# Last quarter of the second MLP product: weight-block sums formed by VectorE ahead of time and out of place, VectorE in program order from there on

## Chip, cores and metric

The kernel runs on one core of one Trainium2 chip. The metric is the device time of one execution in microseconds (us), as the median of the runs; lower is better.

## What is computed

One decoder layer on 512 tokens of width 1024, in fp32. After three token-mixer branches, the layer ends in an MLP with a squared ReLU, a residual sum and a last RMSNorm; only this end matters here:

```
hm = _rmsnorm(x, g_mlp)
x = x + jnp.square(jax.nn.relu(hm @ w_mlp_in)) @ w_mlp_out      # 1024 -> 4096 -> 1024
return _rmsnorm(x, g_final)
```

## The kernel before

**Precision.** Each fp32 matmul is done as three matmuls on parts: an operand is split into `hi` (ScalarE copies it, rounded, to a matmul format) and `lo` (VectorE subtracts: operand minus `hi`). `split_w` does this for weights (tiles `whi`, `wlo`, 128x1024 each, four buffers of each) and `stationary` for activations (`shi`, `slo`).

**The second MLP product** is cut into four quarters of the 4096 hidden channels (`prods[0]` to `prods[3]`). A quarter multiplies a 512x1024 activation block by a 1024x1024 weight block with seven block products in place of eight (`Product7`). The weight blocks are b11, b12, b21, b22 (`self.b[kh, nh]`, 128x4x512 each, tiles `wq`), loaded by DMA from SyncE's queue (SP). The seven products are issued in the order of `STEPS`: M1, M2, M5, M6, M7, M4, M3. M5 needs the weight sum t1 = b11+b12, M6 needs t2 = t1+b22, M7 needs t3 = b12+b22, M4 needs t4 = t2+b21; M1, M2, M3 take b11, b21, b22 as they are. M5, M6, M7 and M3 also need sums of activation blocks (tiles `u`, `sq`).

**PSUM banks.** Each product fills two banks (e = 0, 1). M1, M6, M7 and M4 pile up in the same pair "x", M2 has the pair "y", M5 and M3 the pair "z". After each product VectorE adds the bank into the residual `x2` (`add`; in the trace `x<-x,ps`). So the first matmul of M7 waits until VectorE has read what the bank held after M6, and the same holds for M4 after M7. M3, the last product, is computed in three pieces: bank e = 0, then the columns 0 to 255 and then 256 to 511 of bank e = 1, and each piece is added when it is done; the last piece waits for the add of the piece before it.

**Order of the work.** A product is two `parts` (kh = 0, 1: half of the weight block each). The list `parts` is worked through in order: the matmuls of part i are emitted, then the splits of part i+4. Between the products of quarters 0 to 2 stand parts of the first MLP product (`in_part`, 24 matmuls each), which need little of VectorE; in the last quarter there are none, and the 14 parts of `prods[3]` follow each other. A scheduler then decides where an engine's instruction stands in its order, unless it is pinned (`V.pin`, helper `_Engine`, line 95: every VectorE, ScalarE and GpSimd instruction has that line).

**Weight sums before.** In quarters 0 to 2 VectorE forms the sums in place in `prep`, one 128x2048 add each (`wq<-wq`). In the last quarter (`self.queue`) GpSimd's queue issues accumulating DMAs instead (`accumulate`, line 1010): they read a block from DRAM and add it to a block that lies in SBUF. One for t3 (on b12), two for t2, one for t1 (on b11, after M1's split), one for t4 (on t2, after M6's split).

**The end.** `final` (called by `add` for a quarter of the output at a time) squares the first half of a row on ScalarE with a sum (`jk`), folds it into `ss` on VectorE, and multiplies that half by the gain on GpSimd (`x<-x,gbf`). For the second half: ScalarE squares it (`hnx<-x`), VectorE completes `ss`, GpSimd takes the power -1/2 (`rsf`), ScalarE and VectorE scale the two halves, and SP stores them.

Of the kernel before, what the change touches and what calls it, by code (L numbers as in the profile page):

```python
# [11 lines left out]
F32 = mybir.dt.float32  # L12
F32R = mybir.dt.float32r
AF = mybir.ActivationFunctionType
ALU = mybir.AluOpType
AX = mybir.AxisListType

P = 128
# [121 lines left out]
def hybrid_block(ctx: ExitStack, tc: tile.TileContext, x, mem, g_mix, w_in, b_gate, conv_w, conv_b,  # L140
                 w_rg_a, b_rg_a, w_rg_x, b_rg_x, lru_lambda, w_lru_out, rel_bias, w_dil_out, g_mem,
                 w_mem_kv, w_mem_out, w_out, g_mlp, w_mlp_in, w_mlp_out, g_final, onehot, headsel, out):
    nc = tc.nc
# [403 lines left out]
    k0 = qk_proj(0, "k")  # L547
# [440 lines left out]
    class Product7:  # L988
# [3 lines left out]

        def __init__(self, w, k0, queue):
            self.queue = queue
            self.w, self.k0, self.b, self.ps, self.n = w, k0, {}, {}, 0

        def block(self, kh, nh):

            return cols(self.w, nh * 512, 512, self.k0 + kh * 4, 4)

        def load(self, kh, nh):
            b = self.b[kh, nh] = ml.tile([P, 4, 512], F32, name="wq", tag=f"wq{kh}{nh}")
            nc.sync.dma_start(b, self.block(kh, nh))
            if self.queue and (kh, nh) == (0, 1):
                self.accumulate(b, 1, 1)

        def accumulate(self, dst, kh, nh):
            nc.gpsimd.dma_start(out=dst, in_=self.block(kh, nh), accum_op=ALU.add)  # L1010

        def load_sum(self):

            self.t2 = raw_tile(4, 512)
            nc.sync.dma_start(self.t2, self.block(0, 0))
            self.accumulate(self.t2, 0, 1)
            self.accumulate(self.t2, 1, 1)

        def stationary(self, src):
            i, self.n = self.n, self.n + 1  # L1020
# [14 lines left out]
        def prep(self, p, sq):  # L1035

            b11 = self.b[0, 0]
            a11, a21 = (sq[0][:, :, h * 256:(h + 1) * 256] for h in range(2))
            if p == 1:
                self.stat = self.stationary(a11)  # L1040
                return b11
            b12, b21, b22 = (self.b.get(k) for k in ((0, 1), (1, 0), (1, 1)))
            a12, a22 = (sq[1][:, :, h * 256:(h + 1) * 256] for h in range(2))
            if p == 5:
                self.u = self.sums()
                V.tensor_sub(self.u, a21, a22)
                if not self.queue:
                    V.tensor_add(b11, b11, b12)
                act, w = self.u, b11
            elif p == 6:  # L1050
                u, self.u = self.u, self.sums()
                V.tensor_sub(self.u, u, a11)
                if self.queue:
                    b11 = self.t2
                else:
                    V.tensor_add(b11, b11, b22)
                act, w = self.u, b11
            elif p == 7:
                V.tensor_sub(a11, a11, a21)
                if not self.queue:  # L1060
                    V.tensor_add(b12, b12, b22)
                act, w = a11, b12
            elif p == 4:
                if self.queue:
                    b11 = self.t2
                else:
                    V.tensor_add(b11, b11, b21)
                act, w = a22, b11
            elif p == 3:
                V.tensor_add(self.u, self.u, a12)  # L1070
                act, w = self.u, b22
            else:
                act, w = a12, b21
            self.stat = self.stationary(act)
            return w
# [6 lines left out]
        def parts(self, n, sq, done, free):  # L1082


            p, bank, opens, (th, nh), sign = self.STEPS[n]
            last = n == 6 and done is not None
            now = {}

            def split(kh):
                if kh == 0:  # L1090
                    now["w"] = self.prep(p, sq)
                    now["a"] = self.stat
                now[kh] = split_w(now["w"][:, 2 * kh:2 * kh + 2, :], 2, 512)
                if kh == 1:
                    free(p)
                    if self.queue and p == 1:
                        self.accumulate(self.b[0, 0], 0, 1)
                    if self.queue and p == 6:
                        self.accumulate(self.t2, 1, 0)

            def mult(e, kh, c0, c1):
                (ah, al), (whi, wlo) = now["a"], now[kh]
                o = self.ps[bank, e][:, c0:c1]
                sl = slice(e * P, (e + 1) * P)
                for kk in range(2):
                    k = 2 * kh + kk
                    hi, lo = whi[:, kk, c0:c1], wlo[:, kk, c0:c1]
                    more = {"skip_group_check": not opens}
                    PE.matmul(o, ah[:, k, sl], hi, start=opens and k == 0, stop=False, **more)  # L1109
                    PE.matmul(o, ah[:, k, sl], lo, start=False, stop=False, **more)  # L1110
                    PE.matmul(o, al[:, k, sl], hi, start=False, stop=k == 3, **more)  # L1111

            def add(e, c0=0, c1=512):
                t = 2 * th + e
                v = x2[t][:, nh * 512 + c0:nh * 512 + c1]
                (V.tensor_add if sign > 0 else V.tensor_sub)(v, v, self.ps[bank, e][:, c0:c1])
                if done is not None and p in (2, 3, 7, 4):
                    done(t, nh, c0, c1)

            def multiply(kh):  # L1120
                if kh == 0 and opens:
                    for e in range(2):
                        self.ps[bank, e] = psum()
                if last:
                    if kh == 1:
                        for e, c0, c1 in ((0, 0, 512), (1, 0, 256), (1, 256, 512)):
                            mult(e, 0, c0, c1)
                            mult(e, 1, c0, c1)
                            add(e, c0, c1)
                    return  # L1130
                for e in range(2):
                    mult(e, kh, 0, 512)
                    if kh == 1:
                        add(e)

            return [(lambda kh=kh: split(kh), lambda kh=kh: multiply(kh)) for kh in range(2)]
# [49 lines left out]
    def in_part(q, n):  # L1186
        now = {}

        def split():
            m, e = q * 4 + n // 2, n % 2  # L1190
            now["w"] = split_w(raws[m][:, :, e * P:(e + 1) * P], KT, P)
            if e == 1:
                load_in(m + 2)
                if m == 14:
                    prods[3].load_sum()

        def multiply():
            ps = psum()
            mm3(ps, now["w"], hmmov, KT)
            hidden(q, n, ps)  # L1200
            if q == 0 and n in (2, 3, 4, 5):
                prods[0].load(*LOADS[n - 2])

        return now, split, multiply
# [5 lines left out]
    parts = [in_part(0, n)[1:] for n in range(2, 8)]  # L1210
    for q in range(4):
        def free(p, q=q):
            for b in FREE.get(p, ()) if q < 3 else ():
                prods[q + 1].load(*b)


        tiles = (2, 2, 1, 1, 1, 1, 0) if q == 2 else (1, 1, 1, 1, 1, 1, 2) if q < 2 else (0,) * 7
# [14 lines left out]
    for split, _ in parts[2:4]:  # L1232
        split()
    for i, (_, multiply) in enumerate(parts):
        multiply()
        if i + 4 < len(parts):
            parts[i + 4][0]()
# [27 lines left out]
```

## Time and profile before

| what | value |
|---|---|
| time of the runs | 875.82, 875.84, 877.86 us (median 875.84) |
| the profiled execution: its own time | 877.66 us |
| the profiled execution: its span | 875.8 us (1.86 us of its time lie outside) |
| TensorE busy | 855.3 us, 98% of the span |
| VectorE busy | 547.4 us, 63% |
| ScalarE busy | 387.8 us, 44% |
| mean granted TensorE clock | 0.991 |

TensorE (PE) is busy in nearly all of the span, so an engine that is idle elsewhere costs nothing there; what can still change is where TensorE waits, and how long the work after its last matmul takes. A row of a timeline gives the start, the duration, the engine and line, the operation with its tiles, and in brackets how long the engine was idle before and which instruction ended that. An instruction's duration reaches a little past the start of the next one on the same engine.

### The profile page before, as it was taken

How to read it: one execution, taken by the hardware profiler on the slowest of the kernel's cores; microseconds unless marked ns; L12 is line 12 of the kernel's file. 1: busy time of each engine (PE TensorE's matmuls, PEld its weight loads, DVE VectorE, ACT ScalarE, POOL GpSimd, SP SyncE). 2: the span in 40 equal slices, each digit the busy share in tenths (PEclk: the TensorE clock that was granted, in tenths of full speed). 3: DMA queues.
4: the chain of work that ended last, by engine and by line, in shares of the span. 5: the costliest groups of instructions: out<-in, count | busy, mean ns of one | idle time of the engine just before them, and what ended most of it. 6: DMA issues, size and time to landing. Idle time of an engine off the chain costs nothing.

```text
span 875.8 us, 10542 instructions
## 1 busy us (share of the span) xinstructions
PE 855.3 (98%) x4275; PEld 716.7 (82%) x4275; DVE 547.4 (63%) x700; ACT 387.8 (44%) x585; POOL 34.0 (4%) x39
## 2 busy tenths in 40 slices
PE   8899999999999999999999999999999999999986
PEld 7688888889888888888888889888888888888865
DVE  5769666764769642442523446488678856866785
ACT  5457566663654532242332225344425433444444
POOL 3110000000000000000000000000000000001022
PEclk9899999999999999999999999999999999999989
DMA  7583333215332232242325436512531442229522
GB/s 242 170 253 97 97 97 97 97 62 178 98 97 65 80 116 76 72 145 73 96 73 192 144 96 198 163 49 71 170 96 49 145 145 56 88 94 223 116 49 96
DMA packets 82332, 101.16 MB, mean 115 GB/s; under 512 B 3707, under 2 KB 64199, under 8 KB 82156
## 3 DMA queue, kind: packets, MB, share of 16 engines
q1 hardware_dynamic: 78444, 89.20, 32.3%
q0 software_dynamic: 3696, 10.77, 5.4%
q8 instruction: 33, 0.54, 0.3%
q10 hardware_dynamic: 144, 0.52, 0.2%
q14 instruction: 15, 0.12, 0.0%
HBM read 97.32 MB, written 5.52 MB: 117 GB/s over the span
## 4 chain that ended last, share of the span: by engine, by line
PE 85%; DVE 5%; DMA 4%; issue 2%; ACT 2%; POOL 0%; SPq 0%; POOLq 0%; ACTq 0%; DVEq 0%
PE ps L196 19%; PE ps L197 18%; PE ps L198 18%; PE ps L1109 4%; PE ps L1110 4%; PE ps L1111 4%; DMA wq<-in_w_mlp_out_dram 2%; DVE wlo L95 2%; PE ps L944 2%; PE ps L943 2%; PE ps L945 2%; PE ps L518 1%; PE ps L519 1%; PE ps L520 1%; DMA x<-in_x_dram 1%
## 5 line engine op out<-in xcount | busy, mean ns | idle before, releaser
L95 DVE TENSOR_TENSOR wlo<-raw,whi 128x1024 fp32r<-128x1024 f32 (+1 forms) x125 | 147.6, 1186 | 160.8 <-ACT whi L95 156.5
L95 ACT ACTIVATE whi<-raw 128x1024 fp32r<-128x1024 f32 (+1 forms) x126 | 129.4, 1030 | 230.9 <-PE ps L197 158.6
L196 PE MATMUL ps<-hT_hi,whi 128*128 128x512 f32 x400 | 156.6, 392 | 0.0
L197 PE MATMUL ps<-hT_lo,whi 128*128 128x512 f32 x400 | 155.8, 390 | 0.0
L198 PE MATMUL ps<-hT_hi,wlo 128*128 128x512 f32 x400 | 155.7, 389 | 0.0
L95 DVE TENSOR_TENSOR wlo<-wq,whi 128x1024 fp32r<-128x1024 f32 x52 | 65.3, 1257 | 59.5 <-ACT whi L95 59.5
L95 ACT ACTIVATE whi<-wq 128x1024 fp32r<-128x1024 f32 x52 | 54.9, 1058 | 102.4 <-PE ps L197 51.2
L1109 PE MATMUL ps<-whi,shi 128*128 128x512 f32 (+1 forms) x228 | 89.3, 392 | 5.6 <-DVE x L95 5.6
L197 PE MATMUL ps<-hmT_lo,whi 128*128 128x512 f32 x240 | 93.4, 389 | 0.0
L198 PE MATMUL ps<-hmT_hi,wlo 128*128 128x512 f32 x240 | 93.4, 389 | 0.0
L196 PE MATMUL ps<-hmT_hi,whi 128*128 128x512 f32 x240 | 93.2, 389 | 0.0
L1110 PE MATMUL ps<-wlo,shi 128*128 128x512 f32 (+1 forms) x228 | 88.8, 390 | 0.0
L1111 PE MATMUL ps<-whi,slo 128*128 128x512 f32 (+1 forms) x228 | 88.4, 388 | 0.0
L196 PEld LDWEIGHTS ps<-hT_hi,whi 128*128 128x128 f32 x400 | 75.1, 188 | 16.2 <-issue 0.6
L198 PEld LDWEIGHTS ps<-hT_hi,wlo 128*128 128x128 f32 x400 | 75.1, 188 | 15.7
L197 PEld LDWEIGHTS ps<-hT_lo,whi 128*128 128x128 f32 x400 | 75.1, 188 | 15.1
L1109 PEld LDWEIGHTS ps<-whi,shi 128*128 128x128 f32 x228 | 43.5, 191 | 15.5 <-issue 4.6
L198 PEld LDWEIGHTS ps<-hmT_hi,wlo 128*128 128x128 f32 x240 | 45.1, 188 | 9.4
L197 PEld LDWEIGHTS ps<-hmT_lo,whi 128*128 128x128 f32 x240 | 45.1, 188 | 9.3
L196 PEld LDWEIGHTS ps<-hmT_hi,whi 128*128 128x128 f32 x240 | 45.0, 188 | 9.2
L1110 PEld LDWEIGHTS ps<-wlo,shi 128*128 128x128 f32 x228 | 43.5, 191 | 8.7
L1111 PEld LDWEIGHTS ps<-whi,slo 128*128 128x128 f32 x228 | 43.3, 190 | 8.8
(254 smaller groups left out, 1353.2 us busy)
## 6 DMA issues: line engine op xcount, KB each, us to landing
raw<-in_w_in_dram SPq DMA_DIRECT2D x23, 1024.0 KB
raw<-in_w_mlp_in_dram SPq DMA_DIRECT2D x16, 1024.0 KB
wq<-in_w_mlp_out_dram SPq DMA_DIRECT2D x16, 1024.0 KB
raw<-in_w_in_dram SPq DMA_DIRECT2D x12, 512.0 KB
raw<-in_w_mem_kv_dram SPq DMA_DIRECT2D x4, 1024.0 KB
raw<-in_w_out_dram SPq DMA_DIRECT2D x4, 1024.0 KB
x<-in_x_dram SPq DMA_DIRECT2D x7, 512.0 KB
raw<-in_w_lru_out_dram SPq DMA_DIRECT2D x4, 768.0 KB
```

The lines of the kernel that those rows point to most:

```text
L95: r = fn(*a, **k)
L196: PE.matmul(ps, whi[:, k0 + k, :], ah, start=k == 0, stop=False)
L197: PE.matmul(ps, whi[:, k0 + k, :], al, start=False, stop=False)
L198: PE.matmul(ps, wlo[:, k0 + k, :], ah, start=False, stop=k == nk - 1)
L518: PE.matmul(ps[:, 0:256], ah, hi[:, k % 4, :], start=k == 0, stop=False)
L519: PE.matmul(ps[:, 0:256], ah, lo[:, k % 4, :], start=False, stop=False)
L943: PE.matmul(ps, ah[:, sl], hi[:, k % 2, :], start=k == 0, stop=False)
L944: PE.matmul(ps, ah[:, sl], lo[:, k % 2, :], start=False, stop=False)
L945: PE.matmul(ps, al[:, sl], hi[:, k % 2, :], start=False, stop=k == KT - 1)
L1109: PE.matmul(o, ah[:, k, sl], hi, start=opens and k == 0, stop=False, **more)
L1110: PE.matmul(o, ah[:, k, sl], lo, start=False, stop=False, **more)
L1111: PE.matmul(o, al[:, k, sl], hi, start=False, stop=k == 3, **more)
```

## The change

In the last quarter the five accumulating DMAs and the second load of b11 are gone. VectorE forms the four sums instead, each into a tile of its own or into b12, and all of them while the third quarter's last products run: `block_sums(0)` (t1, t3) when M4 of the third quarter has been split, `block_sums(1)` (t2) when the last part of the first MLP product has been split, `block_sums(2)` (t4) when M3 of the third quarter has been split. b22 is loaded earlier, into a spare activation buffer (`wx`). Besides, VectorE's instructions are pinned in program order over the last 14 parts; inside `final` they are not.

```diff
-        def load(self, kh, nh):
-            b = self.b[kh, nh] = ml.tile([P, 4, 512], F32, name="wq", tag=f"wq{kh}{nh}")
+        def load(self, kh, nh, dst=None):
+            b = self.b[kh, nh] = dst or ml.tile([P, 4, 512], F32, name="wq", tag=f"wq{kh}{nh}")
             nc.sync.dma_start(b, self.block(kh, nh))
-            if self.queue and (kh, nh) == (0, 1):
-                self.accumulate(b, 1, 1)
-
-        def accumulate(self, dst, kh, nh):
-            nc.gpsimd.dma_start(out=dst, in_=self.block(kh, nh), accum_op=ALU.add)
-
-        def load_sum(self):
-
-            self.t2 = raw_tile(4, 512)
-            nc.sync.dma_start(self.t2, self.block(0, 0))
-            self.accumulate(self.t2, 0, 1)
-            self.accumulate(self.t2, 1, 1)
+
+        def block_sums(self, step, dst):
+            b11, b12, b21, b22 = (self.b[k] for k in ((0, 0), (0, 1), (1, 0), (1, 1)))
+            if step == 0:
+                self.t1, self.t3 = dst, b12
+                V.tensor_add(dst, b11, b12)
+                V.tensor_add(b12, b12, b22)
+            elif step == 1:
+                self.t2 = dst
+                V.tensor_add(dst, self.t1, b22)
+            else:
+                self.t4 = dst
+                V.tensor_add(dst, self.t2, b21)
...
                 if kh == 1:
                     free(p)
-                    if self.queue and p == 1:
-                        self.accumulate(self.b[0, 0], 0, 1)
-                    if self.queue and p == 6:
-                        self.accumulate(self.t2, 1, 0)
...
                 if done is not None and p in (2, 3, 7, 4):
+                    pin, V.pin = V.pin, False
                     done(t, nh, c0, c1)
+                    V.pin = pin
...
                 load_in(m + 2)
-                if m == 14:
-                    prods[3].load_sum()
+                if m == 15:
+                    prods[3].block_sums(1, raw_tile(4, 512))
...
         def free(p, q=q):
-            for b in FREE.get(p, ()) if q < 3 else ():
+            if q == 2 and p == 7:
+
+                prods[3].load(1, 1, ml.tile([P, 4, 512], F32, name="wx", tag="sq", bufs=4))
+            for b in FREE.get(p, ()) if q + (p == 3) < 3 else ():
                 prods[q + 1].load(*b)
+            if q == 2 and p == 4:
+                prods[3].block_sums(0, raw_tile(4, 512))
+            if q == 2 and p == 3:
+                prods[3].block_sums(2, ml.tile([P, 4, 512], F32, name="wx", tag="sq", bufs=4))
...
     for i, (_, multiply) in enumerate(parts):
+        V.pin = i >= len(parts) - 14
         multiply()
```

What this does to VectorE's order is seen at three places. In the rows, `x2_4030`, `x2_4032`, `x2_4034`, `x2_4036` are the four 128-token blocks of the residual, and the numbers tell tiles apart.

First, VectorE before, from the last split of a first-MLP weight (`wlo_6223`) on, while the third quarter ends:

```order
L95 TENSOR_TENSOR wlo_6223<-raw_5922,whi_6221 128x1024
L95 TENSOR_TENSOR wlo_6259<-wq_5664,whi_6257 128x1024
L95 TENSOR_TENSOR sq_6101<-sq_6101 128x512
L95 TENSOR_TENSOR wlo_6275<-wq_5664,whi_6273 128x1024
L95 TENSOR_TENSOR x2_4034<-x2_4034,ps_5819 128x512
```

The same place in the changed kernel (`wq_6200` is b11, `wq_6128` b12, `wx_6126` b22, `wq_6202` b21):

```order
L95 TENSOR_TENSOR wlo_6223<-raw_5922,whi_6221 128x1024
L95 TENSOR_TENSOR raw_6204<-wq_6200,wq_6128 128x2048
L95 TENSOR_TENSOR wlo_6261<-wq_5664,whi_6259 128x1024
L95 TENSOR_TENSOR wq_6128<-wq_6128,wx_6126 128x2048
L95 TENSOR_TENSOR raw_6225<-raw_6204,wx_6126 128x2048
L95 TENSOR_TENSOR sq_6097<-sq_6097 128x512
L95 TENSOR_TENSOR wlo_6277<-wq_5664,whi_6275 128x1024
L95 TENSOR_TENSOR wx_6279<-raw_6225,wq_6202 128x2048
L95 TENSOR_TENSOR x2_4034<-x2_4034,ps_5819 128x512
```

Four 128x2048 sums have come in between the same splits and adds.

Second, VectorE before, between the splits of M6 and the first add of M6 (`x2_4030<-x2_4030,ps_6371`, which M7's first matmul waits for); `slo_6482` and `wlo_6487`, `wlo_6505` belong to M7, `slo_6520` and `wlo_6525` to M4:

```order
L95 TENSOR_TENSOR wlo_6463<-raw_6072,whi_6461 128x1024
L95 TENSOR_SCALAR ss0_0_6444<-ss0_0_6444 128x1
L95 TENSOR_TENSOR slo_6482<-sq_5884,shi_6481 128x1024
L95 TENSOR_SCALAR ss0_1_6456<-ss0_1_6456 128x1
L95 TENSOR_TENSOR wlo_6487<-wq_6130,whi_6485 128x1024
L95 TENSOR_TENSOR x2_4034<-x2_4034,ps_6466 128x512
L95 TENSOR_TENSOR x2_4036<-x2_4036,ps_6467 128x512
L95 TENSOR_TENSOR wlo_6505<-wq_6130,whi_6503 128x1024
L95 TENSOR_TENSOR slo_6520<-sq_6101,shi_6519 128x1024
L95 TENSOR_TENSOR x2_4030<-x2_4030,ps_6371 128x512
```

In the changed kernel M6's splits end with `wlo_6464`, and M6's first add is `x2_4030<-x2_4030,ps_6372`:

```order
L95 TENSOR_SCALAR ss0_0_6445<-ss0_0_6445 128x1
L95 TENSOR_TENSOR x2_4032<-x2_4032,ps_6415 128x512
L95 TENSOR_SCALAR ss0_1_6457<-ss0_1_6457 128x1
L95 TENSOR_TENSOR wlo_6464<-raw_6225,whi_6462 128x1024
L95 TENSOR_TENSOR sq_5884<-sq_5884 128x4x256
L95 TENSOR_TENSOR slo_6482<-sq_5884,shi_6481 128x1024
L95 TENSOR_TENSOR wlo_6487<-wq_6128,whi_6485 128x1024
...
L95 TENSOR_TENSOR wlo_6505<-wq_6128,whi_6503 128x1024
L95 TENSOR_TENSOR slo_6520<-sq_6097,shi_6519 128x1024
L95 TENSOR_TENSOR wlo_6525<-wx_6279,whi_6523 128x1024
L95 TENSOR_TENSOR x2_4030<-x2_4030,ps_6372 128x512
```

The two `ss0` steps now stand between and behind the adds of M2, the activation sum `sq_5884` stands right ahead of the `slo_6482` that is made from it, and M4's first weight split `wlo_6525` stands ahead of M6's first add; left out are the two adds of M5.

Third, VectorE before in M3, from the last scaling of block 3 on (`x2_4030<-x2_4030,ps_6466` adds the piece e = 0, the 128x256 adds the two pieces of e = 1):

```order
L95 SCALAR_TENSOR_TENSOR hnx_6630<-x2_4036,rsf_6634,gbf_4367 128x512
L95 TENSOR_TENSOR x2_4030<-x2_4030,ps_6466 128x512
L95 TENSOR_TENSOR x2_4032<-x2_4032,ps_6467 128x256
L95 SCALAR_TENSOR_TENSOR ss0_0_6444<-s1_6654,ss0_0_6444 128x1
L95 SCALAR_TENSOR_TENSOR hnx_6653<-x2_4030,rsf_6657,gbf_4367 128x512
L95 TENSOR_TENSOR x2_4032<-x2_4032,ps_6467 128x256
```

The same place in the changed kernel:

```order
L95 SCALAR_TENSOR_TENSOR hnx_6630<-x2_4036,rsf_6634,gbf_4367 128x512
L95 TENSOR_TENSOR x2_4030<-x2_4030,ps_6466 128x512
L95 SCALAR_TENSOR_TENSOR ss0_0_6445<-s1_6654,ss0_0_6445 128x1
L95 SCALAR_TENSOR_TENSOR hnx_6653<-x2_4030,rsf_6657,gbf_4367 128x512
L95 TENSOR_TENSOR x2_4032<-x2_4032,ps_6467 128x256
L95 SCALAR_TENSOR_TENSOR ss0_1_6457<-s1_6677,ss0_1_6457 128x1
L95 TENSOR_TENSOR x2_4032<-x2_4032,ps_6467 128x256
```

The first 128x256 add now stands behind the finishing of block 0 (`ss0_0`, `hnx_6653`).

## Rows read from the trace of the kernel before

**Rows 1.** The page: busy time of TensorE, share of the span, instructions.
```profile
PE 855.3 (98%) x4275; PEld 716.7 (82%) x4275; DVE 547.4 (63%) x700; ACT 387.8 (44%) x585; POOL 34.0 (4%) x39
```

**Rows 2.** TensorE's waits from 560 us on: us in total, times, longest.
```profile
PE ps L1109 <- DVE x L95: 5.6, 2, 4.3
```

**Rows 3.** Timeline of TensorE, last quarter.
```profile
842.97 0.39 PE L1111 MATMUL ps<-whi,slo 128*128 128x512 f32 x1
847.61 0.77 PE L1109 MATMUL ps<-whi,shi 128*128 128x512 f32 x1 [4.25 <-DVE x L95]
...
853.04 0.39 PE L1110 MATMUL ps<-wlo,shi 128*128 128x512 f32 x1
...
866.92 0.39 PE L1109 MATMUL ps<-whi,shi 128*128 128x256 f32 x1 [1.33 <-DVE x L95]
```

**Rows 4.** Windows: length, busy time (instructions) of each engine, clock, DMA share, GB/s.
```profile
804.80:829.20 24.40, 24.40 (x110) 20.20 (x109) 15.40 (x17) 11.37 (x12) 1.27 (x1) 1.00 0.71 162
829.20:847.60 18.40, 14.16 (x63) 11.42 (x62) 18.23 (x20) 8.32 (x11) 4.60 (x3) 0.96 0.33 58
845.00:850.00 5.00, 2.39 (x6) 1.93 (x7) 3.02 (x4) 1.64 (x2) 0.00 (x0) 0.60 0.55 100
```

**Rows 5.** SP's timeline: loads of b12 and of b11.
```profile
788.63 0.37 SPq L1005 DMA_DIRECT2D wq<-in_w_mlp_out_dram  x1
...
799.51 0.37 SPq L1005 DMA_DIRECT2D wq<-in_w_mlp_out_dram  x1
```

**Rows 6.** GpSimd's timeline: an accumulating DMA, a multiplication of `final`.
```profile
794.07 1.30 POOL L1010 DMA_DIRECT2D wq<-in_w_mlp_out_dram  x1 [1.58 <-DMA wq<-in_w_mlp_out_dram]
...
837.72 2.05 POOL L95 TENSOR_TENSOR x<-x,gbf 128x512 f32<-128x512 f32 x1 [17.85 <-ACT jk L95]
```

**Rows 7.** VectorE's timeline: a weight sum; the end of the third quarter; first add of M1.
```profile
778.89 2.28 DVE L95 TENSOR_TENSOR wq<-wq 128x2048 f32<-128x2048 f32 x1
...
818.93 1.22 DVE L95 TENSOR_TENSOR u<-sq 128x1024 f32<-128x1024 f32 x1
...
829.20 1.28 DVE L95 TENSOR_TENSOR x<-x,ps 128x512 f32<-128x512 f32 x2
```

**Rows 8.** ScalarE's timeline: M1's first split behind b11's load; a split behind an activation sum.
```profile
811.93 1.06 ACT L95 ACTIVATE whi<-wq 128x1024 fp32r<-128x1024 f32 x1 [2.82 <-DMA wq<-in_w_mlp_out_dram]
...
820.19 1.06 ACT L95 ACTIVATE shi<-u 128x1024 fp32r<-128x1024 f32 x1 [0.20 <-DVE u L95]
```

**Rows 9.** VectorE's timeline: up to M6's first add, and the split after it.
```profile
838.59 2.26 DVE L95 TENSOR_TENSOR slo<-sq,shi 128x1024 fp32r<-128x1024 f32 x1
...
840.84 2.57 DVE L95 TENSOR_TENSOR wlo<-wq,whi 128x1024 fp32r<-128x1024 f32 x1
843.33 1.27 DVE L95 TENSOR_TENSOR x<-x,ps 128x512 f32<-128x512 f32 x2
844.53 1.21 DVE L95 TENSOR_TENSOR wlo<-wq,whi 128x1024 fp32r<-128x1024 f32 x1
845.66 1.21 DVE L95 TENSOR_TENSOR slo<-sq,shi 128x1024 fp32r<-128x1024 f32 x1
846.80 0.67 DVE L95 TENSOR_TENSOR x<-x,ps 128x512 f32<-128x512 f32 x1
849.45 1.23 DVE L95 TENSOR_TENSOR wlo<-raw,whi 128x1024 fp32r<-128x1024 f32 x1 [1.98 <-ACT whi L95]
```

**Rows 10.** VectorE's timeline: the end.
```profile
859.82 0.67 DVE L95 TENSOR_TENSOR x<-x,ps 128x512 f32<-128x512 f32 x1
861.34 0.16 DVE L95 SCALAR_TENSOR_TENSOR ss<-s,ss 128x1 f32<-128x1 f32 x1 [0.85 <-ACT hnx L95]
862.16 0.75 DVE L95 SCALAR_TENSOR_TENSOR hnx<-x,rsf,gbf 128x512 f32<-128x512 f32 x1 [0.67 <-POOL rsf L95]
...
865.86 1.01 DVE L95 TENSOR_TENSOR x<-x,ps 128x512 f32<-128x512 f32 x2
...
870.68 0.75 DVE L95 SCALAR_TENSOR_TENSOR hnx<-x,rsf,gbf 128x512 f32<-128x512 f32 x1 [0.66 <-POOL rsf L95]
```

More of the change, by code (lines that the diff above doesn't have):

```diff
@@ L988, in hybrid_block, with __init__ @@
     class Product7:
-        def __init__(self, w, k0, queue):
-            self.queue = queue
+        def __init__(self, w, k0, last):
+            self.last = last
             self.w, self.k0, self.b, self.ps, self.n = w, k0, {}, {}, 0
@@ L1046, in prep @@
                 V.tensor_sub(self.u, a21, a22)
-                if not self.queue:
+                if not self.last:
                     V.tensor_add(b11, b11, b12)
-                act, w = self.u, b11
+                act, w = self.u, self.t1 if self.last else b11
             elif p == 6:
@@ L1052, in prep @@
                 V.tensor_sub(self.u, u, a11)
-                if self.queue:
-                    b11 = self.t2
-                else:
+                if not self.last:
                     V.tensor_add(b11, b11, b22)
-                act, w = self.u, b11
+                act, w = self.u, self.t2 if self.last else b11
             elif p == 7:
                 V.tensor_sub(a11, a11, a21)
-                if not self.queue:
+                if not self.last:
                     V.tensor_add(b12, b12, b22)
@@ L1063, in prep @@
             elif p == 4:
-                if self.queue:
-                    b11 = self.t2
-                else:
+                if not self.last:
                     V.tensor_add(b11, b11, b21)
-                act, w = a22, b11
+                act, w = a22, self.t4 if self.last else b11
             elif p == 3:
```

## The prediction, as it was put on record

> **What bounds the kernel now.** First the page: TensorE is busy in 98% of the span [rows 1], so work on another engine counts only where TensorE waits for it, or behind the last matmul. Then TensorE's waits in the last 316 us: two, 5.6 us together, both for a VectorE add [rows 2]. The timeline shows where: 4.25 us before M7's first matmul and 1.33 us before the last piece of M3 [rows 3]. Behind the first one the granted clock is 0.60 in the window from 845 to 850 us, which mixes the half level (1.2 GHz) with the full one, and the pace is back only by 853.04 [rows 3, 4]. Last, VectorE itself: from 829.20 to 847.60 it is busy for 18.23 of 18.40 us [rows 4]. So the tail is VectorE's chain of instructions, worked through in order, and I price the change by walking that chain before and after. The marks are the starts of four adds: M1's first (829.20), M6's first (846.80), M3's first (865.86) and the last scaling (870.68) [rows 7, 9, 10]; 5.1 us of span follow the last mark in both kernels.
>
> **Unit prices.** What counts in a chain is the distance to the next start: 1.14 us for a 128x1024 operation (845.66 to 846.80), 0.60 for a 128x512 add (two from 843.33 to 844.53) [rows 9], 2.20 for a 128x2048 sum, its 2.28 less the same overlap of 0.08 [rows 7]. Three round trips matter when nothing stands between their ends in VectorE's order. Activation sum, ScalarE's split, VectorE's `slo`: the sum starts at 818.93, the split ends at 821.25, VectorE itself would be free 1.14 after its start, so it idles 1.2 us [rows 7, 8]. Add, ScalarE's square, `ss`: 0.85 us of idling. `ss`, GpSimd's power, VectorE's scaling: 0.67 [rows 10].
>
> **The change, part by part.**
>
> *The loads.* b11 is still requested when M4 of the third quarter has been split, at 799.51 [rows 5]. Before, ScalarE got it at 811.93, 12.4 us later, with accumulating DMAs under way [rows 8]. b12's load had the DMA engines nearly to itself: requested at 788.63, the accumulate that waits for it starts at 794.07, at most 5.4 us later [rows 5, 6]. Those are the bounds. Without the accumulates nothing else is queued at 800 us, so I take 5.3 us: b11 is there at 804.8. b12, b21 and b22 are requested before it.
>
> *The sums.* The first sum needs b11, and VectorE works in order, so its chain starts at 804.8. Up to M1's first add it holds four sums (8.8 us), ten 128x1024 splits and sums (11.4) and six 128x512 operations (3.6): 23.8 us, plus one activation round trip of 1.2 (`u_6386` is followed directly by its `slo_6389`). M1's first add starts at 829.8, 0.6 us later than before. What hides the 8.8 us is idle time of VectorE: it worked for only 15.40 of the 24.40 us in this stretch [rows 4]. That cover is nearly used up, and each further microsecond would count in full. **+0.6**
>
> *The order up to M6's first add.* Before, this takes 17.6 us: ten 128x1024 operations, six adds, two `ss` steps are 15.1, and the other 2.5 are two operations stretched from 1.22 to 2.26 and 2.57 [rows 9], beside GpSimd's multiplications of `final` [rows 6]. After, it holds eleven 128x1024 operations, because M4's split `wlo_6525` now stands ahead of the add: 16.3. To that come waits that the pinned order makes. `u_6428` is followed directly by `slo_6431`: 1.2. Each `ss0` now stands right behind the add whose square it needs: twice 0.85. `sq_5884` stands directly ahead of `slo_6482`; before, six instructions lay between: 1.2. Of GpSimd's two multiplications the first now falls on VectorE's wait for the second square, the other stretches `wlo_6464` by about 1.2. Together 21.6 us, so M6's first add starts at 851.4 instead of 846.80 and M7's first matmul, 0.81 behind it as before, at 852.2 instead of 847.61. TensorE reaches that point as early as before or a little later (M6's second half waits about 1.5 us for the stretched `wlo_6464`), so its idle time before M7 is some 7 us, not 4.25. **+4.0**
>
> On that stretch the Trainium skill has a rule (SBUF — State Buffer, § SBUF: two separate sides): a VectorE operation with two SBUF inputs and a GpSimd operation that reads SBUF exclude each other for a whole instruction. By it a GpSimd multiplication of 2.05 us could hold VectorE for all of that; the first stretched row lost 1.04. With 2.05 at each of the two places where I charge 1.2, the sum would be 1.7 us higher; I go by the rows.
>
> *M6's first add to M3's first add.* Before 19.1 us. After: five 128x1024 operations, six adds, four `ss` steps and two scalings are 10.9. Waits: one activation round trip (1.2); `wlo_6564`, whose `whi` needs the buffer that M7's first half gives back (M7 starts at half rate, 0.43 us a matmul, so about 1.4); `ss0_2`, whose square stands on ScalarE behind a split that waits for M7's second half (about 1.6); `ss0_3` (0.85); one GpSimd multiplication (1.2); twice square and power for blocks 2 and 3 (3.1). Together 20.3. The 1.98 us that VectorE lost before to the last accumulate [rows 9] are gone, but these waits stand in their place. **+1.2**
>
> *The last piece of M3.* Before, the 128x256 add that frees the bank follows M3's first add by 0.60 [rows 10]. After, `ss0_0` and `hnx_6653` stand between, with both their round trips: 0.60 + 0.85 + 0.08 + 0.67 + 0.67 = 2.9. **+2.3**. Before that piece TensorE then idles about 5.5 us, longer than the 4.25 that were followed by half rate, so I charge its twelve 128x256 matmuls half rate, 0.22 for 0.12 us, 1.2 in all, less 0.2 for an add that no longer stands behind a scaling. **+1.0**
>
> *At no cost:* GpSimd's five DMA issues and the second read of b11 off SP's queue; nobody waited for either on this chain except as named.
>
> Sum: 0.6 + 4.0 + 1.2 + 2.3 + 1.0 = 9.1 us. The profiled execution took 877.66 (span 875.8), so a like one would take 886.8; it is one of the slower of the executions shown. On the median of 875.84 the sum gives **885.0 us**.
>
> **Rivals.**
>
> *The waits shrink, the kernel gets faster.* The mechanism is VectorE's order itself: if ScalarE and GpSimd answer while VectorE still has other work, only the instruction times are left. M6's first add would start at 828.6 + 16.3 = 844.9, 1.9 us earlier than before; TensorE's idle time of 2.3 us might then leave the clock at full, and M7, M4 and M3 would run at TensorE's pace (48 and 18 matmul times of 0.227 us from 845.7 to 860.7), the last scaling near 865.3: 870.5 us. It decides at the pairs: of some 17 us of waits that I count from 829.8 on, about 9 would have to vanish before the change breaks even. For it speaks that before, idle VectorE time is short there. Against it, the order puts sum and `slo`, add and `ss` next to each other, and a ScalarE split alone takes 1.06 [rows 8]. Chance 0.07; near no change, with half of the waits gone, 0.04.
>
> *b11 arrives as late as before.* Then the chain starts at 811.9 and not at 804.8, and as it has no slack left all 7.1 us count: 892.1. For it: that is the only load of b11 that the trace shows. Against it: what filled the DMA engines then (share 0.71 over that stretch [rows 4]) is what the change removes. Chance 0.08.
>
> *The dearer estimates fail.* GpSimd's multiplications fall on gaps (2.4 us less) and TensorE is not slowed at half rate behind its stalls (1.2 for the last piece, about 2 for M7): 885.0 - 5.6 = 879.4. For it: two of four multiplications are already charged nothing; the 1.33 us wait was not followed by half rate [rows 3]. Against it: the stalls grow past the one that was. Chance 0.15.
>
> **How the numbers follow.** My forecast (883 to 888 us) has 0.66, the three others 0.11, 0.08 and 0.15. The range leaves out the first rival and most of the second, 0.19 together: 879.4 to 890.0. A measurement of this kernel tells a change from none at about 0.3%, 2.6 us. Slower by more: 0.66 + 0.08 + 0.15 = 0.89; same 0.04; faster 0.07.
>
> **What would show it.** In the changed kernel's trace: the first 128x2048 sum starts near 804.8, directly behind its DMA; M1's first add near 829.8; TensorE's wait before M7 near 7 us, ended by `x<-x,ps`, and M7 starting near 852; short VectorE waits for ScalarE behind `u`, `sq` and the adds; a wait before the last piece of 5 us or more. I am wrong if M7 starts before 848, if the sums run past 820, or if the 128x256 add does not wait for GpSimd's power.

## The result, and the profile after

The changed kernel takes 885.72 us in the median of four runs (885.20 to 886.22), the kernel before 876.75 in the four that ran beside it: ratio 1.0106, 95% interval 1.0090 to 1.0121, so 9 us slower. The forecast was 885.0, in a range from 879.4 to 890.0. The profiled execution took 885.2 us, with a span of 883.2.

The page of the changed kernel: busy time of the engines, against [rows 1].

```profile
PE 854.6 (97%) x4275; PEld 716.5 (81%) x4275; DVE 556.0 (63%) x704; ACT 388.0 (44%) x585; POOL 24.1 (3%) x34
```

VectorE has 8.6 us more work, which is about the four sums (2.28 us each), and TensorE's work is the same within 0.7 us. TensorE's waits from 560 us on, against [rows 2]:

```profile
PE ps L1102 <- DVE x L95: 12.8, 2, 7.4
PE ps L1103 <- DVE wlo L95: 1.3, 1, 1.3
```

Still two waits for an add of VectorE, but 12.8 us instead of 5.6; the third is for a weight split. TensorE's timeline shows the places, which answer to [rows 3]:

```profile
840.98 0.50 PE L1103 MATMUL ps<-wlo,shi 128*128 128x512 f32 x1 [1.31 <-DVE wlo L95]
850.90 0.76 PE L1102 MATMUL ps<-whi,shi 128*128 128x512 f32 x1 [7.36 <-DVE x L95]
...
873.68 0.58 PE L1102 MATMUL ps<-whi,shi 128*128 128x256 f32 x1 [5.43 <-DVE x L95]
```

The second half of M6 waits for the stretched `wlo`, M7 waits 7.36 us in place of 4.25, the last piece of M3 5.43 in place of 1.33. Two windows that answer to [rows 4], the second from M1's first add to M6's first add of this kernel:

```profile
804.80:829.20 24.40, 24.40 (x109) 20.19 (x108) 23.27 (x22) 11.08 (x12) 0.00 (x0) 1.00 0.00 1
828.05:850.07 22.02, 14.19 (x62) 11.09 (x60) 17.69 (x20) 10.43 (x13) 2.59 (x2) 0.95 0.00 1
```

Around M1's first add VectorE went from 15.40 to 23.27 us of 24.40: the sums filled its idle time. (The first window has the times of [rows 4], while M1's first add is at 828.05 here; the 24.40 us that end there have the same 23.27.) In the second window VectorE is busy for 17.69 of 22.02 us, where before it was busy for nearly all of that stretch, 18.23 of 18.40: now it waits. The DMA share is 0.00 where it was 0.71 and 0.33.

VectorE's timeline of the changed kernel, the rows that answer to [rows 7, 9, 10]:

```profile
800.47 1.22 DVE L95 TENSOR_TENSOR wlo<-raw,whi 128x1024 fp32r<-128x1024 f32 x1
803.07 2.29 DVE L95 TENSOR_TENSOR raw<-wq 128x2048 f32<-128x2048 f32 x1 [1.38 <-DMA wq<-in_w_mlp_out_dram]
...
825.77 1.23 DVE L95 TENSOR_TENSOR slo<-u,shi 128x1024 fp32r<-128x1024 f32 x1 [1.13 <-ACT shi L95]
...
828.05 1.28 DVE L95 TENSOR_TENSOR x<-x,ps 128x512 f32<-128x512 f32 x2
...
833.20 1.23 DVE L95 TENSOR_TENSOR slo<-u,shi 128x1024 fp32r<-128x1024 f32 x1 [1.60 <-ACT shi L95]
...
836.95 0.15 DVE L95 TENSOR_SCALAR ss<-ss 128x1 f32<-128x1 f32 x1 [0.79 <-ACT jk L95]
837.02 0.68 DVE L95 TENSOR_TENSOR x<-x,ps 128x512 f32<-128x512 f32 x1
838.51 0.15 DVE L95 TENSOR_SCALAR ss<-ss 128x1 f32<-128x1 f32 x1 [0.81 <-ACT jk L95]
838.58 2.35 DVE L95 TENSOR_TENSOR wlo<-raw,whi 128x1024 fp32r<-128x1024 f32 x1
840.85 1.21 DVE L95 TENSOR_TENSOR sq<-sq 128x1024 f32<-128x1024 f32 x1
843.19 1.23 DVE L95 TENSOR_TENSOR slo<-sq,shi 128x1024 fp32r<-128x1024 f32 x1 [1.13 <-ACT shi L95]
...
850.07 1.28 DVE L95 TENSOR_TENSOR x<-x,ps 128x512 f32<-128x512 f32 x2
...
870.20 0.68 DVE L95 TENSOR_TENSOR x<-x,ps 128x512 f32<-128x512 f32 x1
871.72 0.16 DVE L95 SCALAR_TENSOR_TENSOR ss<-s,ss 128x1 f32<-128x1 f32 x1 [0.84 <-ACT hnx L95]
872.54 0.75 DVE L95 SCALAR_TENSOR_TENSOR hnx<-x,rsf,gbf 128x512 f32<-128x512 f32 x1 [0.66 <-POOL rsf L95]
873.21 0.42 DVE L95 TENSOR_TENSOR x<-x,ps 128x256 f32<-128x256 f32 x1
...
878.47 0.75 DVE L95 SCALAR_TENSOR_TENSOR hnx<-x,rsf,gbf 128x512 f32<-128x512 f32 x1 [0.66 <-POOL rsf L95]
```

Start times of two traces can't be compared directly: how much time lies ahead of the changed part varies from trace to trace by up to 2.8 us. So each mark is counted from a row that all kernels have just ahead of the changed part, the last split of a first-MLP weight (`wlo<-raw`, here 800.47). In the kernel before that row is

```profile
801.89 1.22 DVE L95 TENSOR_TENSOR wlo<-raw,whi 128x1024 fp32r<-128x1024 f32 x1
```

Counted so, the four marks of the prediction went from 27.31 to 27.58 us (M1's first add), from 44.91 to 49.60 (M6's first add), from 63.97 to 69.73 (M3's first add) and from 68.79 to 78.00 (last scaling). Stretch by stretch the change costs +0.3, +4.4, +1.1 and +3.4 us, 9.2 together; the medians differ by 9.0.

The same in one view, VectorE's waits from M1's first add to the end of the changed kernel:

```profile
DVE ss L95 <- ACT jk L95: 4.0, 4, 1.5
DVE slo L95 <- ACT shi L95: 3.9, 3, 1.6
DVE ss L95 <- ACT hnx L95: 3.7, 5, 0.8
DVE hnx L95 <- POOL rsf L95: 2.6, 4, 0.7
DVE x L95 <- PE ps L1104: 2.2, 1, 2.2
DVE wlo L95 <- ACT whi L95: 0.9, 1, 0.9
```

Waits of the kinds in the first two lines, 7.9 us, do not exist on this stretch of the kernel before.

### The profile page after: what moved, and what is told of

The parts are those of the page before. It is cut to its first block, busy times and chain, and to the rows that moved or that the text cites. A ratio compares the mean times of both kernels' runs of the same rounds, so it can differ in the third digit from the quotient of the medians.

```text
span 883.2 us, 10527 instructions
## 1 busy us (share of the span) xinstructions
PE 854.6 (97%) x4275; PEld 716.5 (81%) x4275; DVE 556.0 (63%) x704; ACT 388.0 (44%) x585; POOL 24.1 (3%) x34
## 4 chain that ended last, share of the span: by engine, by line
PE 85%; DVE 5%; DMA 4%; ACT 3%; issue 2%; SPq 1%; POOL 0%; POOLq 0%; ACTq 0%; DVEq 0%
PE ps L196 18%; PE ps L198 18%; PE ps L197 18%; PE ps L1102 5%; PE ps L1103 5%; PE ps L1104 5%; DMA raw<-in_w_in_dram 4%; DVE wlo L95 2%; PE ps L945 2%; PE ps L944 2%; PE ps L943 2%; PE ps L518 1%; PE ps L520 1%; PE ps L519 1%; ACT whi L95 1%
## 5 line engine op out<-in xcount | busy, mean ns | idle before, releaser
L1102 PE MATMUL ps<-whi,shi 128*128 128x512 f32 (+1 forms) x228 | 89.2, 393 | 12.8 <-DVE x L95 12.8
L95 ACT ACTIVATE whi<-wq 128x1024 fp32r<-128x1024 f32 x48 | 50.8, 1059 | 96.3 <-PE ps L197 52.4
L95 DVE TENSOR_TENSOR wlo<-wq,whi 128x1024 fp32r<-128x1024 f32 x48 | 58.6, 1223 | 48.8 <-ACT whi L95 48.8
```

The source lines that it names most:

```text
L95: r = fn(*a, **k)
```

## The experiments

My theory was that the pinned order costs the time, by waits on ScalarE's answers, and that the sums are hidden. The main rival was that the sums cost it. All kernels in one table; the ratio is to the kernel before as it ran beside each of them, with its 95% interval, and the last four columns are the marks, counted from the row named above.

| kernel | median us | ratio | M1 add | M6 add | M3 add | last scaling |
|---|---|---|---|---|---|---|
| before | 876.75 | 1 | 27.31 | 44.91 | 63.97 | 68.79 |
| changed | 885.72 | 1.0106 (1.0090 to 1.0121) | 27.58 | 49.60 | 69.73 | 78.00 |
| 1 sums, no pin | 875.98 | 0.9991 (0.9980 to 1.0002) | 25.29 | 44.11 | 61.47 | 68.60 |
| 2 pin, no sums | 889.50 | 1.0148 (1.0131 to 1.0165) | 29.89 | 53.34 | 73.45 | 81.71 |
| 3 last piece | 882.64 | 1.0063 (1.0049 to 1.0078) | 27.65 | 49.60 | 70.23 | 75.61 |
| 4 activation sums early | 885.60 | 1.0097 (1.0081 to 1.0114) | 27.50 | 47.91 | 68.78 | 77.05 |
| 5 one more sum | 888.29 | 1.0136 (1.0113 to 1.0159) | 29.86 | 52.25 | 73.11 | 81.37 |
| 6 ss0 later | 882.31 | 1.0068 (1.0051 to 1.0085) | 27.64 | 47.68 | 67.60 | 75.56 |
| 7 no GpSimd multiplication | 882.50 | 1.0072 (1.0055 to 1.0089) | 27.58 | 48.47 | 68.55 | 76.73 |
| 8 M4's split later | 885.21 | 1.0098 (1.0080 to 1.0116) | 27.70 | 47.33 | 68.59 | 76.85 |
| 9 = 1, M4's split later | 871.44 | 0.9950 (0.9935 to 0.9965) | 25.46 | 42.12 | 59.10 | 65.43 |
| 10 = 9, last piece | 871.68 | 0.9954 (0.9940 to 0.9967) | 25.30 | 41.85 | 58.86 | 65.00 |
| 11 before, M4's split later | 875.96 | 1.0003 (0.9990 to 1.0016) | 27.76 | 45.35 | 64.53 | 69.35 |
| 12 = 3 and 6 | 879.81 | 1.0032 (1.0020 to 1.0044) | 27.82 | 47.67 | 67.69 | 73.08 |

What the last column says against the kernel before agrees with the ratios (times 877 us) within 1.6 us. The intervals are 1 to 2 us to either side, so the smaller effects are read from the marks, which are one execution each.

**1 and 2: the two halves of the change.** The sums alone:

```diff
-        V.pin = i >= len(parts) - 14
```

> The changed kernel with its sums, but with VectorE's order left to the scheduler (nothing is pinned). My theory: the loss lies in the waits of the pinned order, not in the 8.8 us of sums; the sums stay hidden, M1's first add starts 0 to 2 us earlier than in the changed kernel, the wait before M7 is 3.5 to 5 us, the wait before the last piece near 1.3 us, and the time is 876 to 879 us, within 2 us of the kernel before. Rival (the sums themselves cost the 9 us, because VectorE must form what DMAs formed before): 884 to 886 us, like the changed kernel.

The time is that of the kernel before (0.9991). TensorE waits 3.46 us before M7 and 1.30 before the last piece, close to the 3.5 and 1.3 that I expected; M1's first add comes 2.3 us earlier than in the changed kernel, a little more than the 0 to 2 that I expected. VectorE's waits from M1's first add on are these:

```profile
DVE x L95 <- PE ps L1104: 5.2, 3, 2.7
DVE wlo L95 <- ACT whi L95: 2.8, 1, 2.8
DVE hnx L95 <- POOL rsf L95: 2.0, 3, 0.7
DVE ss L95 <- ACT hnx L95: 0.6, 2, 0.4
```

Not one wait for `shi` or `jk`: with the same instructions the scheduler puts other work between an activation sum and its `slo`, and between an add and its `ss`, as VectorE's timeline of this kernel shows for M6's `u` and `slo` and for the first add of M2 and its `ss`:

```profile
828.55 1.22 DVE L95 TENSOR_TENSOR u<-u,sq 128x1024 f32<-128x1024 f32 x1
...
830.83 0.68 DVE L95 TENSOR_TENSOR x<-x,ps 128x512 f32<-128x512 f32 x1
831.42 1.22 DVE L95 TENSOR_TENSOR slo<-u,shi 128x1024 fp32r<-128x1024 f32 x1
832.56 0.14 DVE L95 TENSOR_SCALAR ss<-ss 128x1 f32<-128x1 f32 x1
```

The rival that the sums cost the time is out.

The order alone, on the kernel before with its accumulating DMAs:

```diff
+        V.pin = i >= len(parts) - 14
...
+                    pin, V.pin = V.pin, False
                     done(t, nh, c0, c1)
+                    V.pin = pin
```

> The kernel before, with its accumulating DMAs, but with VectorE pinned in program order over the last 14 parts as in the changed kernel. My theory: the pinned order alone brings the loss: the wait before M7 is 7 us or more, the wait before the last piece 5 us or more, and the time 884 to 888 us (by the walk of the chain 1 to 2 us above the changed kernel, since b11's split is as late as before and three rows more wait behind it). Rival (the sums cost the time): 875 to 878 us, as before.

It is 13 us slower, more than the changed kernel and above the 884 to 888 us that I expected. ScalarE's timeline of this kernel shows why:

```profile
826.57 1.06 ACT L95 ACTIVATE whi<-wq 128x1024 fp32r<-128x1024 f32 x1 [4.03 <-DMA wq<-in_w_mlp_out_dram]
827.54 1.04 ACT L95 ACTIVATE shi<-u 128x1024 fp32r<-128x1024 f32 x1
```

The activation split stands behind a weight split that waits 4.03 us for the accumulating DMA of t1, and VectorE, pinned, idles 3.50 us for it ahead of M1's first add. So the loss is the pin's, and with the pin the sums *win* 3.7 us (81.71 to 78.00).

**3: the finishing of block 0 ahead of the 128x256 add.**

```diff
                             mult(e, 1, c0, c1)
-                            add(e, c0, c1)
+                            add(e, c0, c1, False)
+                            if c0 == 0 and e == 1:
+                                finish(0, 0, 512)
+                            if e == 1:
+                                finish(e, c0, c1)
```

(Left out: the helper `finish`, which calls `done` unpinned, and the switch `fin`, which keeps `add` from calling it.)

> The changed kernel, but in M3 the two last adds of e = 0 and of the first half of e = 1 stand next to each other, and block 0 is finished behind them. My theory (the finishing of block 0 ahead of the 128x256 add costs 2.3 us there, and the longer stall 1.0 us of half rate): the wait before the last piece falls from 5.4 to about 3.1 us, and the time by 2.3 us if the last piece still runs at half rate, by 3.3 us if not: 882.4 to 883.4 us. Rival (the end is set by block 0's and block 1's finishing on ScalarE and GpSimd, which only moves behind): no change, 885 to 886 us.

TensorE's timeline of this kernel:

```profile
873.28 0.39 PE L1102 MATMUL ps<-whi,shi 128*128 128x256 f32 x1 [3.06 <-DVE x L95]
```

The wait falls from 5.43 to 3.06 us, nine of the twelve matmuls start at full pace, and from M3's first add to the last scaling it takes 5.4 us, not 8.3. By the medians 3.1 us are back, by the last mark 2.4 (in this execution M3's first add came 0.5 us later, although the edit changes nothing ahead of it): as expected, and the fourth term of the prediction stands.

**4: the activation sums one product earlier.** For M5, for instance:

```diff
+                if self.last:
+                    u5, self.u = self.u, self.sums()
+                    V.tensor_sub(self.u, u5, a11)
+                    self.stat = self.stationary(u5)
+                    return self.t1
...
```

> The changed kernel, but each activation sum of the last quarter is formed one product earlier, so that no sum stands directly ahead of the subtraction that needs its ScalarE split. My theory (four such round trips cost 1.2 us each, two of them ahead of M6's first add, one behind, one ahead of M1's first add): the VectorE waits for the activation splits vanish; M6's first add starts 1.5 to 3 us earlier, the time falls by 1.5 to 4 us: 881.5 to 884 us. Rival (VectorE's idle time there only moves to the next instruction, because other waits, for ScalarE's squares and for TensorE, end as late): less than 0.6 us, 885 to 886 us.

The waits for `shi` are gone, and M6's first add comes 1.7 us earlier. But two rows of VectorE's timeline show what took their place:

```profile
839.38 0.15 DVE L95 TENSOR_SCALAR ss<-ss 128x1 f32<-128x1 f32 x1 [1.67 <-ACT jk L95]
...
857.21 1.23 DVE L95 TENSOR_TENSOR wlo<-wx,whi 128x1024 fp32r<-128x1024 f32 x1 [3.91 <-ACT whi L95]
```

The square's wait grew from 0.81 to 1.67 us, and later VectorE waits 3.91 us for a ScalarE split that starts at 856.11, just behind the twelfth matmul of M7 (855.40); the profile names no releaser for it here, in the changed kernel the same split waits for TensorE. At the end 0.9 us remain by the trace, and the times don't tell it from nothing. My expectation of 1.5 to 4 us failed; the rival's reason, that the idle time moves to the next wait, is nearer.

**5: the cover of the sums.**

```diff
                 V.tensor_add(dst, self.t2, b21)
+                V.tensor_add(dst, self.t2, b21)
```

> The changed kernel with one more 128x2048 sum ahead of M1 (t4 is formed twice, with the same result). My theory (the cover of the sums is used up: VectorE is busy from b11's arrival to M1's first add but for one wait of 1.1 us): the extra 2.2 us count in full in VectorE's chain, M1's first add starts 2.2 us later and the time rises by 2 to 3 us: 887.7 to 888.7 us. Rival (the sums lie in idle time of VectorE and TensorE does not notice them): no change, 885 to 886.5 us.

M1's first add comes 2.3 us later, and the last scaling 3.4; the median rises by 2.6. The sums of the change cost next to nothing only because they just fit: the fifth costs its whole length, and more. The more has a place: ScalarE's `shi` for M6 now stands one weight split later, and those splits, each released by TensorE, stand 2.7 us apart there, so M6's `slo` comes 2.7 us later and not 2.3.

**6: ss0 with the second half.**

```diff
-            V.tensor_scalar(ss0[t], ss0[t], 1.0 / D, EPS, op0=ALU.mult, op1=ALU.add)
             G.tensor_tensor(v, v, gbf[:, nh * 512:(nh + 1) * 512], op=ALU.mult)
...
         o_ = outs[t]
+        if c0 == 0:
+            V.tensor_scalar(ss0[t], ss0[t], 1.0 / D, EPS, op0=ALU.mult, op1=ALU.add)
```

> The changed kernel, but the small VectorE step on the sum of squares of a block's first half (ss0) is emitted with the second half, so that VectorE no longer waits for ScalarE's square between two adds. My theory (these waits lie on the chain: 0.79 and 0.81 us ahead of M6's first add, 1.52 and 0.85 behind it): M6's first add starts 1.6 us earlier, the time falls by 2.5 to 3.5 us: 882.2 to 883.2 us. Rival (VectorE's idle time moves to the next instruction that waits for ScalarE or TensorE): less than 1 us, 884.7 to 886 us.

M6's first add comes 1.9 us earlier, the last scaling 2.4, the median falls by 3.4: these waits lay on the chain, as expected.

**7: without GpSimd's multiplications.**

```diff
-            G.tensor_tensor(v, v, gbf[:, nh * 512:(nh + 1) * 512], op=ALU.mult)
```

> The changed kernel without GpSimd's four multiplications of the first halves by the gain (this part of the computation is left out, so those halves of the output lack the gain). My theory (each multiplication that runs beside a VectorE split stretches it, from 1.22 to 2.35 us, and two of the four do): the two stretched splits go back to 1.22 us, M6's first add starts 1.1 us earlier, M3's first add 2.2 us earlier, the time falls by 2 to 3 us: 882.7 to 883.7 us. Rival (VectorE waits for TensorE anyway and the stretch is hidden): less than 0.7 us, 885 to 886 us.

VectorE's timeline of this kernel, the split that was stretched and two waits behind M6's add:

```profile
837.32 1.22 DVE L95 TENSOR_TENSOR wlo<-raw,whi 128x1024 fp32r<-128x1024 f32 x1
...
855.14 1.23 DVE L95 TENSOR_TENSOR wlo<-wx,whi 128x1024 fp32r<-128x1024 f32 x1 [1.51 <-ACT whi L95]
...
858.72 0.15 DVE L95 TENSOR_SCALAR ss<-ss 128x1 f32<-128x1 f32 x1 [1.76 <-ACT jk L95]
```

The split is back at 1.22 us, and M6's first add comes 1.1 us earlier. Of the second stretch, behind it, little more is won by the trace: the waits on ScalarE there grew from 0.86 to 1.51 and from 1.52 to 1.76, and the last scaling comes 1.3 us earlier. TensorE has a part in this. Two windows from M7's first matmul to the end of its half pace, in the changed kernel and in this one (clock: the last but two, 0.50 of full speed):

```profile
850.90:854.85 3.95, 3.95 (x9) 3.10 (x10) 2.77 (x4) 1.06 (x1) 0.00 (x0) 0.50 0.00 0
848.50:854.19 5.69, 5.68 (x14) 4.43 (x14) 3.95 (x4) 1.20 (x2) 0.00 (x0) 0.50 0.00 0
```

M7 began 1.1 us earlier but ran 1.7 us longer at half pace, which at 0.43 in place of 0.23 us a matmul takes back some 0.8 us (an estimate from these rows). In experiment 4 it was 5.66 us. The median falls by 3.2; of the 1.9 us between that and the mark this trace has 1.3 already before the changed part begins, and the rest stays open.

**8: M4's split behind M6's adds.**

```diff
-        if i + 4 < len(parts):
-            parts[i + 4][0]()
+        n = len(parts) - 4
+        for j in {n - 4: (), n - 3: (n, n + 1)}.get(i, (i + 4,)):
+            if j < len(parts):
+                parts[j][0]()
```

> The changed kernel, but the first split of M4 (slo and one wlo, 2.3 us of VectorE) is emitted behind the adds of M6. My theory (the chain of VectorE as a whole sets the end): M6's first add and M7 start 2.3 us earlier, but the two rows only move behind them, so that of this only the waits for ScalarE's buffers are saved and the time falls by about 1 us: 884.3 to 885.3 us. Rival (what stands ahead of M6's first add is what counts, as my prediction charged the M4 split in its second term): 2.3 us or more, 883.4 us or less.

M6's first add comes 2.3 us earlier, M3's 1.1, the last scaling 1.2, and the median 0.5, within what I expected: what stands ahead of M6's add is only worth in full what doesn't come back behind it.

**9, 10 and 11: can the parts be used?** With the sums in the scheduler's order (1) VectorE waits 5.2 us for TensorE at its end, so there what is moved behind M6's adds should not come back. Kernel 9 is 1 with the edit of 8:

> The sums of the changed kernel in the scheduler's order (as in the first experiment, 875.98 us), and M4's first split emitted behind M6's adds. There the first experiment had VectorE wait 2.79 and 2.69 us later on, so time that is taken from ahead of M6's first add need not come back. My theory: TensorE's wait before M7 falls from 3.46 us to about 1.2, without half rate behind it, and the time by 3 to 5 us: 871 to 873 us, faster than both kernels. Rival (VectorE's chain as a whole sets the end here too, as in the pinned order, where the same edit gave 0.5 us): 875 to 876 us.

TensorE's waits in that kernel:

```profile
PE ps L1102 <- DVE x L95: 2.7, 2, 1.5
PE ps L1102 <- ACT shi L95: 0.4, 1, 0.4
```

The wait before M7 is 1.5 us, and the kernel is faster than both: 0.9950, 871.44 us, as expected. The same edit on the kernel before (11):

> The kernel before, unchanged but for M4's first split, emitted behind M6's adds: tells whether the early M6 add alone brings what it brings together with the sums. My theory: before M6's first add VectorE's order there holds only one split less, and later the accumulating DMA's wait of 2 us stays; the time falls by 0 to 2 us: 874 to 876.5 us. Rival (the early add is worth the same in both): 872 to 873 us.

Its ratio is 1.0003, but it doesn't answer the question. VectorE's timeline of this kernel:

```profile
844.77 1.21 DVE L95 TENSOR_TENSOR slo<-sq,shi 128x1024 fp32r<-128x1024 f32 x1
845.91 0.67 DVE L95 TENSOR_TENSOR x<-x,ps 128x512 f32<-128x512 f32 x1
```

M4's `slo` still stands directly ahead of M6's first add, as in [rows 9], and the other split of M4 stood behind it already. From 790 us on VectorE's, ScalarE's and GpSimd's rows follow each other as in the kernel before: the scheduler put the moved rows back where they were, and M6's first add is at 45.35, not earlier than 44.91. So an early M6 add without the sums is untested; to be moved there is one row of 1.14 us. What is shown is that the sums, a free order and an early M6 add together are faster than the kernel before by some 4 us (0.9950).

Kernel 10 is 9 with the edit of 3, and the last part alone pinned, and brought no more:

```diff
-        V.pin = i >= len(parts) - 14
+        V.pin = i >= len(parts) - 1
```

> The kernel with the early M6 add and the scheduler's order, and besides the last part alone in program order, with block 0 finished between the two last adds of M3 (as in the third experiment). In the first experiment block 0's finishing stood behind the last add, and 7.1 us lay between M3's first add and the last scaling, 4.8 in the kernel before. My theory: these go to about 5.3 us, 1 to 2 us less than without this step: 869.5 to 872 us. Rival (the end is set by the last piece's matmuls and their own finishing): no change against the kernel with the early M6 add alone.

Its 871.68 us lie in my range too, but the rival was right: from M3's first add to the last scaling it takes 6.1 us, where I expected 5.3 and kernel 9 has 6.3. The reason is another than the rival's, as ScalarE's timeline of this kernel shows:

```profile
860.19 0.63 ACT L95 ACTIVATE hnx<-x 128x512 f32<-128x512 f32 x1 [1.46 <-DMA out_dram<-hnx]
```

Block 0's square waits 1.46 us for the store of the block whose `hnx` buffer it takes (there are two). Kernel 9 has the same wait, but there block 0's finishing stands behind the last add; here the last add stands behind block 0's finishing, and so behind that wait. So at this pace the stores of the output may be next; no run here removes that wait.

**12: two repairs in the pinned order.** The edits of 3 and 6 together:

> The changed kernel, pinned as it is, with the two edits together that each gave back over 2 us: ss0 emitted with the second half, and block 0 finished behind the first 128x256 add of M3. My theory: they remove different waits (ScalarE's square between adds; the finishing of block 0 ahead of that add) and add up: 2.4 + 2.4 us by the two traces, a little more where the wait before the last piece falls under the length that was followed by half rate: 879.5 to 881.5 us, so about half of the loss is repaired without giving up the program order. Rival (both shorten the same wait before the last piece and the second adds little): 882 to 883 us.

The last scaling comes 4.9 us earlier than in the changed kernel, 2.4 + 2.4 by the two traces apart; the median is 879.81 us, as expected. Of the loss 2.8 us remain by the ratio and 4.3 by the marks, 2.8 of these ahead of M6's first add.

## Why the prediction was right, point by point

- *b11 and the sums, +0.6.* Right at its mark. b11's first use is at 803.07, 2.6 us behind the common row; forecast 804.8, which in that clock is 2.9. M1's first add comes 0.3 us later. That little of the cover is left is shown by the fifth experiment. The second rival, b11 as late as before, is out. But this term is no cost of its own, which the prediction's unbroken VectorE chain did not see: in the changed kernel and in experiments 3, 6, 7, 8 and 12 M1's first add lies between 27.58 and 27.82, and M6's `slo`, the next row that waits, at 32.72 to 32.74 in all six. What it waits for hangs on TensorE (next point).
- *The order up to M6's first add, +4.0.* Measured +4.4: 22.0 us in place of the forecast 21.6. The waits came where the order put them: 1.60 (forecast 1.2), 0.79 and 0.81 (0.85 each), 1.13 (1.2), and 1.13 of stretch (1.2). The 0.4 us too little is the first: ScalarE's `shi` stood behind a weight split that waits for TensorE, which the prediction saw for `ss0_2` and not here. That M6's first add comes 4.7 us later in all, against the forecast 4.6, is thus in part luck: the first term was 0.3 too dear and this one 0.4 too cheap. ScalarE's timeline of the changed kernel:

```profile
831.16 1.06 ACT L95 ACTIVATE whi<-raw 128x1024 fp32r<-128x1024 f32 x1 [1.66 <-PE ps L1104]
832.13 1.04 ACT L95 ACTIVATE shi<-u 128x1024 fp32r<-128x1024 f32 x1
```

- *M6's first add to M3's first add, +1.2.* Measured +1.1, with 0.86 for the `whi` buffer (forecast 1.4) and 1.52 for the square (1.6).
- *The last piece, +2.3 and +1.0.* Measured +2.4 (873.21 is 3.01 behind 870.20, before 0.60) and +1.0 (from the last piece's first matmul to the last scaling 4.79 us, before 3.76). The third experiment takes both away.
- *GpSimd's multiplications.* Two of the four were charged 1.2 us each, and two stretch a split, by 1.13 and 1.12. What was wrong is the 2.05 us of [rows 6] as the length of a multiplication: where no VectorE split is under way at its start it takes 1.30, as GpSimd's timeline of the changed kernel shows:

```profile
836.99 1.30 POOL L95 TENSOR_TENSOR x<-x,gbf 128x512 f32<-128x512 f32 x1 [303.61 <-ACT jk L95]
838.55 1.29 POOL L95 TENSOR_TENSOR x<-x,gbf 128x512 f32<-128x512 f32 x1 [0.26 <-ACT jk L95]
```

The second holds the split that starts 0.03 behind it for 1.13 us, nearly its whole length. That is what the Trainium skill's rule says (SBUF — State Buffer, § SBUF: two separate sides), and the trace agrees. The 1.7 us more that I worked out from the rule came from the 2.05, which, as I read it, held GpSimd's own wait for VectorE: in the kernel before, the split that began at 837.39 was still under way when this multiplication began at 837.72.

- *What the sum doesn't say.* It adds prices along one chain, and as a forecast of the whole that held. But a price in it is not what its removal gives back: experiments 4 and 8 took 1.7 and 2.3 us away ahead of M6's first add and kept 0.9 and 1.2 at the last mark, and experiment 7, which frees two stretched splits of 1.1 us each, kept 1.3. Behind M6's first add VectorE soon waits for splits on ScalarE whose buffers TensorE frees, so the pace of M7 counts, and its half pace was not equally long (last section).
- *The first rival.* It needed 9 of some 17 us of waits to vanish. The waits and stretched splits that the prediction prices from there to the first 128x256 add come to 16.2 us; the trace has 15.5 in their places. Hardly any vanished. (The six lines above add up to 17.3, but they leave out the two stretches and go on to the end.)

## What to carry to other kernels

Program order is a bad order for an engine whose next instruction needs another engine's answer to its last one: look in the order for pairs such as sum and split, add and square, and charge each a round trip (here 0.8 to 1.6 us) unless other work stands between. Work that is moved into an engine's idle time is nearly free while it fits; past that it can cost more than its length, because the next step is taken at another engine's pace (here 2.2 us of sum cost 2.7). A gain upstream in a chain must be followed to the chain's end, wait by wait, before it is counted.

## What the runs showed of the hardware that I had not expected

How long TensorE stays at half pace (0.43 us from one 128x512 matmul to the next, a granted clock of 0.50, the level of 1.2 GHz) behind an idle stretch does not follow the length of that stretch. Before M7 it was 3.95 us behind 7.36 idle in the changed kernel, 4.84 behind 7.35 in the third experiment with the same instructions there, 5.69 behind 7.32 in the seventh, 6.11 behind 7.03 in the twelfth, 2.7 behind 3.46 in the first, and some 5.2 to 5.4 behind 4.25 in the kernel before [rows 3]. In the third experiment, behind 3.06 us of idling, the last piece began at full pace and fell to half only for its last three matmuls. Each of these is one execution, so the marks behind M7 carry differences that no edit made: M3's first add is at 69.73 in the changed kernel and at 70.23 in the third experiment, whose edit lies behind it.

A VectorE add that reads a PSUM bank was not stretched beside a GpSimd multiplication: the one at 837.02 in the changed kernel, 0.68 us long, lies wholly inside the multiplication from 836.99 to 838.29.
